# Encoder layer on one core: turned softmax weights kept in the score buffers, value products in fours, and later delayed pieces

## The chip, the cores and the metric

One Trainium2 chip, of which one core is used. The metric is device time in microseconds (us), from the start to the end of one execution; three runs of the kernel before gave 1165.29, 1167.19 and 1170.32 us, median 1167.19.

## What is computed

One layer of a bidirectional encoder on 1024 tokens of width 1024. The combined projection feeds two groups of heads, whose outputs are joined and projected; a gated feed-forward part with a per-layer input follows. The change lies in the two groups of heads alone.

```python
u = einsum('bsd,de->bse', x, w_in)
rq, rk, rv, rg, aq, ak, av = split(u)
y_ret = retention(rq, rk, rv, forward and backward decay) -> group norm * gain * silu(rg)   # 8 heads of 64
y_att = windowed_gqa(aq, ak, av, sink)                                                     # 8 heads, 2 kv heads
mix = concat(y_ret, y_att) @ w_out
h = layer_norm(alpha * x + mix)
out = layer_norm(alpha * h + (silu(h @ w_gate) * (h @ w_up)) @ w_down + sigmoid(h @ w_pg) * (p @ w_pe))

# windowed_gqa, for each block of 128 queries and its up to 3 neighbouring blocks of keys
scores = q k / 8 - slope * distance, masked to |distance| <= 128
m = max(scores, sink);  e = exp(scores - m);  denom = sum(e) + exp(sink - m)
y = (e / denom) @ v
```

## The kernel before, in words

**Products.** Every float32 product is made of three matmuls with operands that are split into an upper and a lower part (`mm3`, lines 82 to 84). One such step of 128x512 is called a projection step below.

**The mixers.** After a first stretch that loads x and makes the first four columns of projection tiles, the kernel works on four pairs of retention heads and four pairs of attention heads (one attention head of each kv group, g = 0 and 1). Round 0 is attention pair 0 beside 80 projection steps, and then retention pair 0 beside 48. Rounds 1, 2 and 3 each hold retention pair i and attention pair i beside 48 projection steps; 16 steps with the last value products end the mixers.

**What sets the order.** TensorE's order is written out by hand: `run` goes through a list in which F stands for a share of the projection steps in `queue` (2 or 3 steps in rounds 1 to 3), and every other entry is a section of mixer work. `take` counts the steps; the count is called ticks. Pieces in `later` and `side` are issued when their tick has come: parts of the group norm (`LAGS`: spread, power, store, fetch, scaled), parts of the softmax sums (`LAGA`), and the pieces that split weights of later stages ahead of time (`presplit_gate`, `presplit_out`, `presplit_small`), each a ScalarE copy, one or two VectorE operations and a store. VectorE, ScalarE and the queue of transfers on SyncE are put in order by the scheduler of the tile framework; `behind` keeps a piece from being scheduled ahead of the matmul after which it was issued.

**Attention, by block n of 128 queries.**
- `scores(n)`: for each g two matmuls into a bank of the kind "s" (lines 579, 580), a VectorE operation that adds bias, takes the row minimum and frees the bank (L581), a ScalarE exponential with its row sum (L584). After blocks 3 and 7, `sums` finishes the denominators of four blocks (L591 to L593).
- `turn(n)`: transposes of the weights into a bank of the kind "t" (L619) and a ScalarE copy (L624) into a buffer `ptr`, of which there are four; the turn of block 2 (or 6), g = 1, also transposes the reciprocals of the sums (L622), from where `spread` sends them through device memory and back into `y` (L604, L608).
- `values(n)`: up to six matmuls (L636) into a bank of the kind "o". After block 3 (or 7) VectorE multiplies the bank by what lies in `y` (L639).

**Retention, by pair i.** `keys` transposes and scales keys (L420, L426), `kv` makes the states' increments in two banks of the kind "t" and then two of the kind "s" (L441), which ScalarE and VectorE free (L450, L448); `scan` adds them up on VectorE (L458) and sends them to the tile `states` (L469); `scores` fills both "s" banks (L480), which VectorE frees by a multiplication into the buffer `pt` (L483), the one from which the backward states are sent; `queries` is L494, `out` lines 506 and 511, `norm` lines 530 to 551.

There are two banks of each kind, used in turn. So a section that fills "s" banks waits until the section before it that did so has been freed.

## Time and profile before

| | |
|---|---|
| three runs, median (lowest to highest) | 1167.19 us (1165.29 to 1170.32) |
| the profiled execution | 1168.1 us |
| its span, first to last instruction | 1166.3 us |
| granted TensorE clock, mean | 0.998 |
| TensorE busy | 1151.7 us, 99% |
| VectorE busy | 896.7 us, 77% |
| ScalarE busy | 565.0 us, 48% |
| mixers (from the first attention scores to the last value products) | about 55 to 344 us |

A row of the timeline has the start in us from the span's start, the length, the engine (PE is TensorE, DVE VectorE, ACT ScalarE, SPq the queue of transfers), the line, the operation, what is written and read, the shape, and the count; in brackets stands the engine's idle time before it and what ended it. Matmuls overlap, so the pitch from one start to the next says what one costs, not its length.

### The profile page before, as it was taken

How to read it: one execution, taken by the hardware profiler on the slowest of the kernel's cores; microseconds unless marked ns; L12 is line 12 of the kernel's file. 1: busy time of each engine (PE TensorE's matmuls, PEld its weight loads, DVE VectorE, ACT ScalarE, POOL GpSimd, SP SyncE). 2: the span in 40 equal slices, each digit the busy share in tenths (PEclk: the TensorE clock that was granted, in tenths of full speed). 3: DMA queues.
4: the chain of work that ended last, by engine and by line, in shares of the span. 5: the costliest groups of instructions: out<-in, count | busy, mean ns of one | idle time of the engine just before them, and what ended most of it. 6: DMA issues, size and time to landing. Idle time of an engine off the chain costs nothing.

```text
span 1166.3 us, 19077 instructions
## 1 busy us (share of the span) xinstructions
PE 1151.7 (99%) x6978; PEld 966.6 (83%) x6978; DVE 896.7 (77%) x1687; ACT 565.0 (48%) x1162; POOL 103.8 (9%) x118
## 2 busy tenths in 40 slices
PE   9999999999999999999999999999999999999997
PEld 7888877878888888888888888888888888888885
DVE  4656678785959898948999988888888976774777
ACT  5655366767646265214445433443344445552462
POOL 2000010101010020000000000000000011133242
PEclk9999999999999999999999999999999999999999
DMA  7345776666467955766232332232223289999978
GB/s 251 89 169 212 255 250 219 232 203 204 144 221 242 360 182 183 267 199 208 108 103 98 107 116 96 96 136 100 100 73 136 87 252 344 335 246 215 258 169 233
DMA packets 88863, 218.64 MB, mean 187 GB/s; under 512 B 12544, under 2 KB 20928, under 8 KB 88768
## 3 DMA queue, kind: packets, MB, share of 16 engines
q1 hardware_dynamic: 79984, 200.11, 49.5%
q0 software_dynamic: 8784, 17.31, 8.4%
q8 instruction: 55, 0.90, 0.3%
q14 instruction: 40, 0.33, 0.1%
HBM read 143.35 MB, written 62.19 MB: 176 GB/s over the span
## 4 chain that ended last, share of the span: by engine, by line
PE 92%; DMA 3%; DVE 2%; issue 1%; SPq 0%; ACT 0%; POOL 0%; DVEq 0%; ACTq 0%; POOLq 0%
PE bmm L876 8%; PE bmm L877 8%; PE bmm L878 8%; PE bt L876 6%; PE bt L877 6%; PE bt L878 6%; PE bmm L82 5%; PE bmm L83 5%; PE bmm L84 5%; PE bs L877 4%; PE bs L878 4%; PE bs L876 4%; PE bo L878 4%; PE bo L877 4%; PE bo L876 4%; PE bo L636 2%
## 5 line engine op out<-in xcount | busy, mean ns | idle before, releaser
L82 PE MATMUL bmm<-H,w 128*128 128x512 f32 x240 | 97.4, 406 | 0.2
L83 PE MATMUL bmm<-H,w 128*128 128x512 f32 x240 | 94.3, 393 | 0.0
L84 PE MATMUL bmm<-H,w 128*128 128x512 f32 x240 | 94.0, 392 | 0.0
L1476 ACT ACTIVATE ev<-ev 128x512 f32<-128x512 f32 x42 | 26.4, 630 | 105.4 <-DVE ev L1505 92.1
L1650 POOL DMA_DIRECT2D h0b<-in_w_dn x24 | 21.6, 900 | 538.5 <-DVE ev L1456 503.6
L82 PEld LDWEIGHTS bmm<-H,w 128*128 128x128 f32 x240 | 45.1, 188 | 11.7 <-issue 1.2
L84 PEld LDWEIGHTS bmm<-H,w 128*128 128x128 f32 x240 | 45.2, 188 | 10.2
L83 PEld LDWEIGHTS bmm<-H,w 128*128 128x128 f32 x240 | 45.3, 189 | 7.7
L584 ACT ACTIVATE sc<-sc,st 128x384 f32<-128x384 f32 (+1 forms) x64 | 37.3, 586 | 18.7 <-DVE st L581 18.5
L624 ACT ACTIVATE ptr<-bt 128x384 f32<-128x384 f32 (+1 forms) x64 | 26.6, 459 | 29.8 <-PE bt L619 29.7
L581 DVE CUSTOM_DVE_ANT_0 sc<-cst,bs,nskb 128x384 f32<-128x384 f32 (+1 forms) x64 | 35.2, 577 | 7.3 <-PE bs L580 7.0
L1505 DVE TENSOR_TENSOR ev<-ev,bt 128x512 f32<-128x512 f32 x44 | 30.1, 683 | 12.5 <-PE bt L878 12.5
L77 DVE TENSOR_TENSOR w<-raw,w 128x512 fp32r<-128x512 f32 x34 | 23.3, 696 | 19.0 <-ACT w L76 18.7
L1456 DVE TENSOR_TENSOR ev<-ev,bs 128x256 f32<-128x256 f32 x63 | 25.6, 418 | 15.5 <-PE bs L878 14.7
L1478 DVE TENSOR_TENSOR ev<-ev 128x512 f32<-128x512 f32 x42 | 29.0, 691 | 10.5 <-ACT ev L1476 9.0
L876 PE MATMUL bmm<-H,u 128*128 128x512 f32 x92 | 36.1, 392 | 0.0
L877 PE MATMUL bmm<-H,u 128*128 128x512 f32 x92 | 36.0, 392 | 0.0
L878 PE MATMUL bmm<-H,u 128*128 128x512 f32 x92 | 35.8, 389 | 0.0
L876 PE MATMUL bmm<-H,w 128*128 128x512 f32 x84 | 32.9, 392 | 0.0
L877 PE MATMUL bmm<-H,w 128*128 128x512 f32 x84 | 32.9, 392 | 0.0
L878 PE MATMUL bmm<-H,w 128*128 128x512 f32 x84 | 32.7, 389 | 0.0
L1456 DVE TENSOR_TENSOR ev<-ev,bo 128x256 f32<-128x256 f32 x70 | 28.4, 417 | 5.1 <-PE bo L878 4.4
(832 smaller groups left out, 3837.1 us busy)
## 6 DMA issues: line engine op xcount, KB each, us to landing
ad<-ev SPq DMA_DIRECT2D x33, 512.0 KB, 2.6
pgd<-pro SPq DMA_DIRECT2D x28, 512.0 KB, 3.5
raw<-in_w_gu SPq DMA_DIRECT2D x22, 512.0 KB, 4.0
ln<-in_w_gu SPq DMA_DIRECT2D x22, 512.0 KB, 4.5
raw<-ad SPq DMA_DIRECT2D x40, 256.0 KB, 6.1
ln<-ad SPq DMA_DIRECT2D x37, 256.0 KB, 6.5
H<-in_w_dn SPq DMA_DIRECT2D x33, 256.0 KB, 9.1
wod<-aq SPq DMA_DIRECT2D x16, 512.0 KB, 3.0
```

Source lines behind the costliest of these rows:

```text
L82: pe.matmul(o, lh, rh, start=start, stop=False)
L83: pe.matmul(o, lh, rl, start=False, stop=False)
L84: recent[0] = pe.matmul(o, ll, rh, start=False, stop=stop).ins.name
L581: dve.tensor_tensor_reduce(sc[g][:, :nk], cst[:, tc0:tc0 + nk], b[:, :nk], slope(i, g), nskb[:, 2 * i + g:2 * i + g + 1], ALU.add, ALU.min ...
L584: act.activation(sc[g][:, :nk], sc[g][:, :nk], AF.Exp, bias=st_[:, 0, j, g:g + 1], scale=-1.0, accum_out=st_[:, 2, j, g:g + 1])
L624: act.activation(p_[:, :hi - lo, :], tb[:, :hi - lo, :], AF.Copy)
L876: pe.matmul(o, lh, rh, start=start, stop=False, skip_group_check=True)
L877: pe.matmul(o, lh, rl, start=False, stop=False, skip_group_check=True)
L878: pe.matmul(o, ll, rh, start=False, stop=stop, skip_group_check=True)
L1456: dve.tensor_tensor(out_, x, b, ALU.add)
L1478: dve.tensor_tensor(c[:, 1, :], c[:, 0, :], c[:, 1, :], ALU.mult)
L1505: dve.tensor_tensor(get(name), ev[left][:, m, :], right, ALU.add)
```

## The change

Five things are done together.

1. `turn` copies the turned weights back into the buffers of the scores (`self.sc`) from which they were transposed; the buffers `ptr` go, and `NSC` doubles from 4 to 8.
2. Value products stand four blocks together, twice for a pair of heads, where they stood two by two four times. Blocks 4 to 7 are multiplied in the next round, ahead of `kv`. The other entries are set out anew: the first scores now come right behind `kv`, without projection steps between, and the scores of block 4 right behind the retention scores. Round 1, which has no value products to take over, has one more share F.
3. The reciprocals are transposed in the turn of block 3 (or 7), g = 0, one block later, and their fetch follows after 4 ticks instead of 5. The multiplication L639 becomes a piece of `later`, 5 ticks behind the value products (`LAGV`).
4. `scaled` (L551) of retention pair 0 comes 4 ticks later (`LAGX`).
5. Seven pieces of `presplit_gate` start at tick 58.5 instead of 57, and the pieces of `presplit_out(2)` move from ticks 7 to 27.4 to ticks 10 to 28.

```diff
-NSC = 4
-LAGA = (2, 1, 5)
+NSC = 8
+LAGA = (2, 1, 4)
 LAGS = (3, 6, 9, 12, 15)
+LAGX = 4
+LAGV = 5
...
-            later.extend((ticks[0] + at, f) for at, f in zip(LAGS, (spread, power, store, fetch, scaled)))
+            late = 0 if self.i else LAGX
+            later.extend((ticks[0] + at, f) for at, f in zip(LAGS, (spread, power, store, fetch)))
+            later.append((ticks[0] + LAGS[4] + late, scaled))
...
-                last = g and n % 4 == 2
+                last = not g and n % 4 == 3
...
-                p_ = bt([P, 3, P], "ptr", 4)
+                p_ = self.sc[n][g].rearrange("p (k q) -> p k q", q=P)
...
             if j == 3:
-                dve.tensor_tensor(self.half(hh), self.o[hh], self.half(hh), ALU.mult)
+
+                def times():
+                    behind(dve.tensor_tensor(self.half(hh), self.o[hh], self.half(hh), ALU.mult))
+
+                later.append((ticks[0] + LAGV, times))
...
-        at = [2 + 2.8 * k for k in range(14)] + [57 + 2.6 * k for k in range(7)] + [75.5] + [79.5 + 2.4 * k for k in range(7)]
+        at = [2 + 2.8 * k for k in range(14)] + [58.5 + 2.5 * k for k in range(7)] + [75.5] + [79.5 + 2.4 * k for k in range(7)]
...
-                side.extend(presplit_out(2, ops, 2, 3.4, late[:1]))
+                side.extend(presplit_out(2, ops, 2, (10, 13, 16, 19, 22, 25, 28), late[:1]))
...
-            run([K(0), F, K(1), *([] if V else [F]), sco(0), F, *V, C(0), C(1), F, sco(1), S_(0, 0), F, trn(0), sco(2), S_(0, 1), F, trn(1),
-                 sco(3), S_(1, 0), F, val(0), val(1), S_(1, 1), F, trn(2), sco(4), F, trn(3), sco(5), Q(0), F, val(2), val(3),
-                 (r.scores,), F, trn(4), sco(6), Q(1), F, trn(5), sco(7), F, (r.out,), E(0), E(1), F, G[0], F, M(0), G[1], F,
-                 val(4), val(5), G[2], F, trn(6), M(1), F, trn(7), F], 48)
-            V = [val(6), val(7)]
+            run([K(0), F, K(1), F, *([] if V else [F]), *V, C(0), C(1), sco(0), F, sco(1), S_(0, 0), F, trn(0), sco(2), S_(0, 1), F,
+                 trn(1), sco(3), S_(1, 0), F, trn(2), S_(1, 1), F, trn(3), Q(0), F, val(0), val(1), val(2), val(3),
+                 (r.scores,), sco(4), Q(1), F, sco(5), F, trn(4), sco(6), F, trn(5), sco(7), F, (r.out,), E(0), E(1), F, G[0], F,
+                 M(0), G[1], F, trn(6), G[2], F, trn(7), M(1), F], 48)
+            V = [val(4), val(5), val(6), val(7)]
```

The list of round 0 is rearranged in the same manner. In the rows of the changed kernel below, lines are up to 8 higher than before (L480 is L482, L483 is L485, L579 is L583, L636 is L640).

**First place: TensorE at the retention scores of round 1.** The retention scores fill the two "s" banks (2063 and 2064 before, 2003 and 2004 after). Before, two projection steps and a turn stand behind them:

```order
L480 MATMUL bs_2063<-rq_1465,rk_1206 64x64
L480 MATMUL bs_2064<-rq_1465,rk_1206 64x64
L82 MATMUL bmm_2039<-H_96,w_1669 128x512
L83 MATMUL bmm_2039<-H_96,w_1669 128x512
L84 MATMUL bmm_2039<-H_96,w_1669 128x512
L82 MATMUL bmm_2039<-H_165,w_1669 128x512
L83 MATMUL bmm_2039<-H_165,w_1669 128x512
L84 MATMUL bmm_2039<-H_165,w_1669 128x512
L619 MATMUL bt_2105<-cst,sc_1978 128x128 x3
L619 MATMUL bt_2111<-cst,sc_1979 128x128 x3
L579 MATMUL bs_2119<-k_411,aq_468 128x384
```

and after the change the scores of block 4 follow at once, in the next use of the same two banks:

```order
L482 MATMUL bs_2003<-rq_1449,rk_1190 64x64
L482 MATMUL bs_2004<-rq_1449,rk_1190 64x64
L583 MATMUL bs_2042<-k_411,aq_468 128x384
L584 MATMUL bs_2042<-kz_413,aq_468 128x384
L583 MATMUL bs_2046<-k_412,aq_1577 128x384
L584 MATMUL bs_2046<-kz_414,aq_1577 128x384
L84 MATMUL bmm_2056<-H_96,w_1653 128x512
```

What moved: all work that lay between filling both banks and needing them again now stands behind the second use. Rounds 2 and 3 have the same order there.

**Second place: VectorE ahead of freeing those banks, round 1.** These are the last rows before the two multiplications that free the banks (`qq`, `rb` and `kv` are scaled queries, `pre` and `pro` pieces of `presplit_gate`). Before:

```order
L656 TENSOR_TENSOR pro_1139<-pre_1134,pro_1139 128x512
L494 TENSOR_TENSOR qq_2025<-rq_1379,qd_1602 128x512 x2
L717 TENSOR_TENSOR pre_1135<-pre_1135,pre_1134 128x512
L494 TENSOR_TENSOR rb_2129<-rq_1465,qd_1602 128x512
L494 TENSOR_TENSOR kv_2130<-rq_1465,qd_1602 128x512
L245 COPY rq_2034<-bmm_1921 64x512
L483 TENSOR_TENSOR pt_2062<-bs_2063,dt_1603 128x512
L656 TENSOR_TENSOR pro_1138<-pre_1135,pro_1138 128x512
L483 TENSOR_TENSOR pt_2062<-bs_2064,dt_1603 128x512
```

and after, where the last wide step of the backward scan (`pt` from `pt`, 128x7x64) stands close ahead too:

```order
L460 SCALAR_TENSOR_TENSOR pt_1769<-pt_1769,cd 128x7x64
L664 TENSOR_TENSOR pro_1122<-pre_1118,pro_1122 128x512
L496 TENSOR_TENSOR qq_1957<-rq_1363,qd_1586 128x512
L725 TENSOR_TENSOR pre_1118<-pre_1119,pre_1118 128x512
L496 TENSOR_TENSOR rb_2052<-rq_1449,qd_1586 128x512
L496 TENSOR_TENSOR kv_2053<-rq_1449,qd_1586 128x512
L664 TENSOR_TENSOR pro_1123<-pre_1118,pro_1123 128x512
L247 COPY rq_1974<-bmm_1900 64x512
L485 TENSOR_TENSOR pt_2002<-bs_2003,dt_1587 128x512
L485 TENSOR_TENSOR pt_2002<-bs_2004,dt_1587 128x512
```

What moved: the four evictions of attention scores that stood between that scan step and the multiplications are gone from there, and seven wide operations lie between.

**Third place: TensorE behind `kv` in round 2.** The last matmuls of `kv` fill the "s" banks (2541 and 2542 before, 2494 and 2493 after). Before, three projection steps follow:

```order
L441 MATMUL bs_2541<-rv_449,pt_2439 64x64 x2
L441 MATMUL bs_2542<-rv_449,pt_2439 64x64 x2
L82 MATMUL bmm_2450<-H_232,w_2269 128x512
L83 MATMUL bmm_2450<-H_232,w_2269 128x512
L84 MATMUL bmm_2450<-H_232,w_2269 128x512
```

and after, the scores of block 0:

```order
L443 MATMUL bs_2493<-rv_449,pt_2390 64x64 x2
L443 MATMUL bs_2494<-rv_449,pt_2390 64x64 x2
L583 MATMUL bs_2531<-k_411,aq_2283 128x256
L584 MATMUL bs_2531<-kz_413,aq_2283 128x256
L583 MATMUL bs_2535<-k_412,aq_2284 128x256
L584 MATMUL bs_2535<-kz_414,aq_2284 128x256
```

What moved: the scores of block 0, which stood ahead of `kv` with a share of projection steps behind them, now take the banks that `kv` has just filled.

More of the change, by code (lines that the diff above doesn't have):

```diff
@@ L803, in layer @@
         run([F, F, sco(0), F, sco(1), F], 16)
-        run([F, (av_turn, 0), (av_turn, 1), F, trn(0), sco(2), F, trn(1), sco(3), F, val(0), val(1), trn(2), sco(4), F,
-             trn(3), sco(5), F, val(2), val(3), trn(4), sco(6), F, trn(5), sco(7), F, val(4), val(5), trn(6), (decay_q, 0),
-             F, trn(7), (decay_k, 0, 0), F, val(6), val(7), (decay_k, 0, 1), F], 64)
-        assert not side and not later
+        run([F, (av_turn, 0), (av_turn, 1), F, trn(0), sco(2), F, trn(1), sco(3), F, trn(2), F,
+             trn(3), F, val(0), val(1), val(2), val(3), sco(4), F, sco(5), F, trn(4), sco(6), F, trn(5), sco(7), F, trn(6), (decay_q, 0),
+             F, trn(7), (decay_k, 0, 0), F, val(4), val(5), val(6), val(7), (decay_k, 0, 1), F], 64)
+        assert not side
         y0 = ytile(0)
```

## The prediction

> **What bounds the kernel now.** I read the page first, then TensorE's waits, then stretches of 10 us over the mixers, then the timeline at each wait.
>
> ```profile
> PE 1151.7 (99%) x6978; PEld 966.6 (83%) x6978; DVE 896.7 (77%) x1687; ACT 565.0 (48%) x1162; POOL 103.8 (9%) x118
> PE bs L579 <- DVE st L581: 3.3, 3, 2.1
> PE bt L622 <- DVE st L593: 1.4, 1, 1.4
> PE bt L441 <- ACT pt L426: 0.7, 1, 0.7
> 180.00:190.00 10.00, 8.04 (x57) 6.26 (x56) 9.24 (x27) 6.83 (x19) 0.00 (x0) 1.00 0.64 221
> 190.00:200.00 10.00, 9.36 (x122) 7.62 (x121) 10.00 (x24) 5.80 (x16) 0.00 (x0) 1.00 0.85 281
> 230.00:240.00 10.00, 7.90 (x158) 6.66 (x155) 6.70 (x14) 5.16 (x14) 0.00 (x0) 1.00 0.58 193
> ```
>
> TensorE is the bound: busy 99% of the span. The change adds no matmul and takes none away. It can win only TensorE's idle time in the mixers, 3.3 + 1.4 + 0.7 = 5.4 us, and the loss where TensorE goes from one kind of section to another. In the stretches (the columns after the length are PE, PEld, DVE, ACT, POOL, clock, DMA share, GB/s) VectorE is full exactly where TensorE waits in round 1: 9.24 and 10.00 of 10 us. Around 235 us it isn't (6.70).
>
> **Joints between sections.** Projection steps run at an even pitch; these rows give what a value section costs beside its matmuls.
>
> ```profile
> 190.28 0.40 PE L82 MATMUL bmm<-H,w 128*128 128x512 f32 x1
> ...
> 191.67 0.82 PE L619 MATMUL bt<-cst,sc 128*128 128x128 f32 x6
> 213.48 0.40 PE L82 MATMUL bmm<-H,w 128*128 128x512 f32 x1
> ...
> 215.64 1.53 PE L636 MATMUL bo<-ptr,av 128*64 128x128 f32 x24
> 217.10 0.50 PE L82 MATMUL bmm<-H,w 128*128 128x512 f32 x1
> ...
> 218.62 0.82 PE L619 MATMUL bt<-cst,sc 128*128 128x128 f32 x6
> 229.31 1.31 PE L636 MATMUL bo<-ptr,av 128*64 128x128 f32 x20
> 230.56 0.64 PE L441 MATMUL bt<-rv,qq 64*64 64x64 f32 x28
> ```
>
> Six matmuls ahead of a turn take 191.67 - 190.28 = 1.39 us, 0.23 each. Nine ahead of values take 215.64 - 213.48 = 2.16, 0.07 over nine such pitches. Twenty-four value matmuls take 1.46 and twenty 1.25, so four cost 0.21, all 24 would cost 1.26, and 0.20 goes at the exit. The six behind them take 1.52, 0.13 too many. A value section thus costs 0.07 + 0.20 + 0.13 = 0.40 us by itself. There are 16 and there will be 8: 3.2 us saved. Against it, 8 turns now end in projection steps and no longer in scores; no row shows this alone, so I bound it by nothing and by the 0.13 above, 1.0 us in all, and take the middle, since the scores then save part of their own entry. Sum: **-2.6 us** (-2.0 to -3.2).
>
> **The waits of before.** There are five.
>
> ```profile
> 170.76 0.45 PE L441 MATMUL bt<-rv,qq 64*64 64x64 f32 x14 [0.67 <-ACT pt L426]
> 179.04 0.75 DVE L551 SCALAR_TENSOR_TENSOR y<-y,gn,rb 128x512 f32<-128x512 f32 x1 [2.26 <-DMA rb<-rnd]
> 181.91 0.44 PE L579 MATMUL bs<-k,aq 128*128 128x384 f32 x1 [0.58 <-DVE st L581]
> 189.47 0.27 PE L622 MATMUL bt<-cst,st 128*8 128x128 f32 x1 [1.38 <-DVE st L593]
> 193.48 0.45 PE L579 MATMUL bs<-k,aq 128*128 128x384 f32 x1 [0.64 <-DVE st L581]
> ```
>
> The 0.67 goes: round 1 gets a share of projection steps ahead of `kv`. The 0.58 came from VectorE, which had stood 2.26 us before L551 for a fetch; 4 ticks of three matmuls at 0.23, 2.8 us, cover that. The 1.38 goes because the reciprocals are transposed a turn later; late next is the same reciprocal, by 0 to 0.5 us. The 0.64 goes because the scores of block 4 no longer come there. Sum: **-3.3 us** (-2.8 to -3.3). The fifth is another matter.
>
> ```profile
> 233.16 0.68 DVE L448 COPY pt<-bs 128x512 f32<-128x512 f32 x1
> ...
> 236.50 0.08 DVE L581 DVE_READ_ACCUMULATOR2_ANT st<- 128x1 f32 x1
> ...
> 237.25 0.45 PE L579 MATMUL bs<-k,aq 128*128 128x384 f32 x1 [2.10 <-DVE st L581]
> q8 instruction: 1, 0.02, 3.8%
> ```
>
> The bank that this matmul takes had been read out by 233.84, and the VectorE operation that the row names ended 0.67 us ahead of the matmul, where the other waits end within 0.1 us of theirs. In the stretch from 234.5 to 236 us a packet of the instruction queue moves (last row; from 230.4 to 234.5 there was none), just behind `kv` with its dense small matmuls. I read it as TensorE short of instructions. The change leaves `kv` where it is but puts the scores, with a wait of their own, into the time in which the instructions come. So it may go or stay: 0 to -2.1, and I take half, **-1.0 us**. The Trainium skill (Runtime: NRT & Kernel Launch, section Instruction fetch mechanics) says that instructions come in blocks of 256 and that crossing a block is "mostly hidden". By that the wait would be VectorE's after all and would go whole, and the sum would be 1.1 us lower; the trace speaks against it with the bank free since 233.84.
>
> **New wait 1: scores right behind `kv`.** In the three rounds block 0 now needs banks that `kv` has just filled.
>
> ```profile
> 172.66 0.50 PE L82 MATMUL bmm<-H,w 128*128 128x512 f32 x1
> ...
> 172.84 0.55 ACT L450 ACTIVATE pt<-bs 128x448 f32<-128x448 f32 x1 [0.30 <-PE bs L441]
> 172.85 0.69 DVE L448 COPY pt<-bs 128x512 f32<-128x512 f32 x1 [0.28 <-PE bs L441]
> ```
>
> `kv` was over at 172.66, and the banks were free at 173.39 and 173.54. The wait is 0.73 with both engines idle; it was hidden by projection steps and now stands open. With 0.05 for the signal: 3 x 0.8 = **+2.4 us** (2.2 to 3.6, the upper end being 0.4 more each, from the copy that came late at 233.16).
>
> **New wait 2: scores right behind the retention scores.** Block 4 needs the two banks that L483 has to free.
>
> ```profile
> 316.03 0.50 PE L82 MATMUL bmm<-H,w 128*128 128x512 f32 x1
> ...
> 316.15 1.29 DVE L483 TENSOR_TENSOR pt<-bs,dt 128x512 f32<-128x512 f32 x2 [0.51 <-PE bs L480]
> 191.61 0.68 DVE L458 SCALAR_TENSOR_TENSOR pt<-pt,cd 128x448 f32<-128x448 f32 x1
> 192.31 1.11 SPq L469 DMA_DIRECT2D states<-pt  x2
> DMA to landing us min/median/max: 3.1/3.3/6.2
> 195.62 1.29 DVE L494 TENSOR_TENSOR qq<-rq,qd 128x512 f32<-128x512 f32 x2
> 196.82 0.69 DVE L717 TENSOR_TENSOR pre<-pre,pre 128x512 f32<-128x512 f32 x1
> ```
>
> With VectorE idle, the second bank is free at 317.44, 1.41 us after the retention scores; the first half of the attention scores fills 0.35 of this (two matmuls of 384 columns, against 0.23 for 512). The floor is 1.1 us a round. But L483 writes the buffer `pt` out of which the backward states are sent, and that is now late. From the end of that scan step (192.29) the two issues take until 193.42, and 3.3 us (median) later the second has landed: 4.5 us. Before, L483 came 7 to 9 us behind the scan step. Now four blocks of values (2.5 us) and the retention scores (1.1) follow a last share of steps, and by the order on VectorE (pitch 0.60 for a wide operation, 196.82 - 195.62 halved) I count the scan's end at about 3.3 us before the retention scores' end in rounds 2 and 3, with two to four wide operations behind it. So L483 starts 1.2 us late: 1.1 + 1.0 = 2.1 each. In round 1 seven wide operations stand between scan and L483: 4.2 us. VectorE has 15 wide and 9 narrow operations, 10.6 us, between the eviction of block 3 and L483, and TensorE's sections take 10.5, with VectorE some 1.6 us behind at their start: L483 starts 1.6 to 1.9 us late, a wait of 2.8. Sum 2.8 + 2.1 + 2.1 = **+7.0 us** (3.3 at the floor; about 12 if transfers take 5 us to land, between median and maximum).
>
> **Costed at nothing.** Copying turned weights in place is the same ScalarE work, and the buffers are as many, 8; block 4's scores need block 0's values, which stand ahead on TensorE itself. The later multiplication L639 covers its fetch in rounds 1 to 3; uncovered, it would hold VectorE some 1 us (included in the range). The 16 last steps still cover the pieces behind the mixers.
>
> **Sum.** -2.6 - 3.3 - 1.0 + 2.4 + 7.0 = +2.5 us. Against the profiled execution (span 1166.3, and 1.8 around it: 1168.1) that is 1170.6; the median of the runs is 0.9 lower, so I say **1169.7 us**: no difference that can be measured, since a measurement of this kernel can tell about 0.5%, 5.8 us, from no change.
>
> **The rivals.**
> - *Floors.* If the states land in time, both new waits stay at their floors, 2.2 + 3.3, and the fifth wait goes: -2.6 - 3.3 - 2.1 + 5.5 = -2.5, 1164.7 us. For it speaks that VectorE has slack over a round; against it the 4.5 us from scan to landing.
> - *Late states, slower than before.* If the transfer of the backward states binds in all three rounds at 5 us rather than 3.3, by stores of pieces ahead of it on the queue (round 1 has 0.85 DMA share at 190 to 200), wait 2 is 12 us and the sum +7.5: 1174.7. It decides from a wait of 3.4 us a round on.
> - *The clock.* TensorE starts slow:
>
> ```profile
> 6.02 0.63 PE L82 MATMUL bt<-H,w 128*128 128x512 f32 x1
> 6.45 0.63 PE L82 MATMUL bo<-H,w 128*128 128x512 f32 x1
> ...
> 7.52 0.39 PE L83 MATMUL bs<-H,w 128*128 128x512 f32 x1
> 7.75 0.40 PE L84 MATMUL bs<-H,w 128*128 128x512 f32 x1
> ```
>
> Its pitch is 0.43 until about 6.9 us and 0.23 after, some 5.6 us of slow work from 1.3 us on. If the wait in round 1 sent it back to that state, 5.6 x (1 - 0.23/0.43) = 2.6 us would come on top: 1172.3. A wait of 2.10 us left the clock at 1.00. The Trainium skill (TensorE: Matmul & The Clock Gate, section Why this matters for your kernels) warns of gaps over about 3 us; no wait here was that long.
> - *It doesn't do what it says.* The three waits for VectorE (2.6) only move: 1172.3.
>
> **Chances.** Forecast 0.55, floors 0.20, late states 0.18, clock 0.04, moved waits 0.03. Faster by over 0.5% 0.03 (the lower edge of the floors), slower 0.20 (late states, and half of the last two rounded), the same 0.77. The range goes from 1163.5 (floors, with joints at -3.2 and half a us of spread) to 1177 (late states with the fifth wait kept).
>
> **What would show it.** In the changed profile: L441 and L622 gone from TensorE's waits (terms of -3.3); 16 value sections become 8; a wait of 0.8 before the first L583 behind L443 in each round; a wait of about 2 to 3 before L583 behind L482, with L485 started late by a transfer of `states`. A floor wait of 1.1 there, or waits over 4, would prove the main term wrong.

## The result, and the profile after

| | before | after |
|---|---|---|
| median of the runs (lowest to highest) | 1165.13 us (1164.79 to 1170.32), 6 runs | 1182.76 us (1181.18 to 1186.25), 6 runs |
| the profiled execution | 1168.1 us | 1181.43 us |
| its span | 1166.3 us | 1179.7 us |
| granted clock, mean | 0.998 | 0.993 |

The ratio is 1.0147, with a 95% interval of 1.0134 to 1.016: the change makes the kernel slower by about 17 us, where 1169.7 us and no measurable difference had been forecast, and the time lies above the range. The profiled executions differ by 13.3 us, since that of before is 3.0 us above its median and that of after 1.3 us below; this account is made with these two.

First the busy line of the page of after:

```profile
PE 1155.0 (98%) x6978; PEld 970.6 (82%) x6978; DVE 896.1 (76%) x1687; ACT 563.7 (48%) x1162; POOL 103.5 (9%) x118
```

and TensorE's largest waits in the mixers of after (engine, what is written, line, the releaser; us in total, times, longest):

```profile
PE bs L583 <- DVE pt L485: 9.2, 3, 3.4
PE bt L626 <- DVE st L597: 2.4, 2, 1.4
PE bs L583 <- ACT pt L452: 2.2, 3, 0.7
PE bt L443 <- ACT pt L428: 0.5, 1, 0.5
PE bt L623 <- ACT sc L628: 0.4, 1, 0.4
```

TensorE has as many matmuls as before, yet is busy 3.3 us longer: some of them ran more slowly. The forecast's two new waits are there, in three rounds each. The first (L452, the copies behind `kv`) was forecast at 2.4 us in all and has 2.2; the second (L485) at 7.0 and has 9.2. The wait for the reciprocals (L626), which was to go, is longer than before: 2.4 us in all, where it was 1.4.

The timeline of after at the three long waits, with what VectorE did: the last row of the backward scan (in round 1 also the transfer's issue, SPq, and VectorE's last operation ahead of the multiplications), the two multiplications that free the banks, the scores of block 4. Rows between are left out.

```profile
191.28 0.67 DVE L460 SCALAR_TENSOR_TENSOR pt<-pt,cd 128x448 f32<-128x448 f32 x1
192.09 1.21 SPq L471 DMA_DIRECT2D states<-pt  x2
195.49 0.68 DVE L247 COPY rq<-bmm 64x512 f32<-64x512 f32 x1
197.43 1.29 DVE L485 TENSOR_TENSOR pt<-bs,dt 128x512 f32<-128x512 f32 x2 [1.27 <-DMA states<-pt]
198.17 0.58 PE L583 MATMUL bs<-k,aq 128*128 128x384 f32 x1 [3.44 <-DVE pt L485]
...
253.00 0.68 DVE L460 SCALAR_TENSOR_TENSOR pt<-pt,cd 128x448 f32<-128x448 f32 x1
258.76 1.29 DVE L485 TENSOR_TENSOR pt<-bs,dt 128x512 f32<-128x512 f32 x2 [1.89 <-DMA states<-pt]
259.50 0.49 PE L583 MATMUL bs<-k,aq 128*128 128x384 f32 x1 [2.42 <-DVE pt L485]
...
316.21 0.68 DVE L460 SCALAR_TENSOR_TENSOR pt<-pt,cd 128x448 f32<-128x448 f32 x1
322.90 1.29 DVE L485 TENSOR_TENSOR pt<-bs,dt 128x512 f32<-128x512 f32 x2 [4.80 <-DMA states<-pt]
323.64 0.44 PE L583 MATMUL bs<-k,aq 128*128 128x384 f32 x1 [3.34 <-DVE pt L485]
```

and the transfers of the tile `states`, from issue to landing:

```profile
DMA to landing us min/median/max: 3.9/4.5/5.2
```

In all three rounds VectorE stood idle ahead of L485, for 1.27, 1.89 and 4.80 us, and the transfer of the backward states out of `pt` ended it: the mechanism of the forecast. In rounds 2 and 3 VectorE was free before the retention scores were done. In round 1 it was late too: it came free at 196.17 us (195.49 + 0.68), 1.4 us behind TensorE's last retention score (198.17 - 3.44 = 194.73), and stood 1.27 us more for the transfer. But the states took longer. From the end of the scan (the start of its row and its length) to the start of L485 it is 5.5, 5.1 and 6.0 us; 4.5 had been counted, with 3.3 us for a transfer. That was the median of before, where the trace has the landing of six of the 16 transfers. In after it has four, and their median is 4.5.

What the forecast's sum lacks shows when the span is cut into stretches of 3.41 us. The columns are the stretch, its length, TensorE's busy time and instructions, the granted clock, DMA share and GB/s. First after, at the three waits, then before, around its wait of 2.10 us:

```profile
194.91:198.32 3.41, 0.15 (x1) 1.00 1.01 351
198.32:201.73 3.41, 3.41 (x10) 0.50 0.40 117
201.73:205.14 3.41, 3.41 (x19) 1.00 0.47 160
...
256.35:259.76 3.41, 0.99 (x53) 1.00 0.86 272
259.76:263.17 3.41, 3.41 (x10) 0.50 0.70 189
...
321.20:324.61 3.41, 0.97 (x4) 1.00 0.06 12
324.61:328.02 3.41, 3.41 (x10) 0.50 0.26 78
```

```profile
232.53:235.94 3.41, 2.61 (x12) 1.00 0.46 178
235.94:239.35 3.41, 2.10 (x11) 1.00 0.62 229
```

Behind each of the three waits TensorE had half its clock for one stretch of 3.41 us: ten matmuls, against 19 in the full stretch that follows the first one. From the start of the first matmul behind the wait to the start of the 31st it is 7.40, 7.77 and 7.91 us, against 6.08, 6.36 and 6.36 in the run with the scans swapped below, which has the same order of matmuls and no such stretch: 4.3 us in all.

So the 13.3 us of the profiled executions are: waits of TensorE before the output projection 14.7 us instead of 5.4, +9.3; half clock +4.3; joints -1.7 (not measured one by one: it is what is left of the 11.87 us by which the output projection starts later, next rows); and 1.5 us behind the mixers.

```profile
354.68 0.39 PE L876 MATMUL bt<-w,H 128*128 128x512 f32 x1
366.55 0.39 PE L884 MATMUL bt<-w,H 128*128 128x512 f32 x1
```

### The profile page after: what moved, and what is told of

Its sections match the earlier page's. It is cut to its first block, busy times and chain, and to the rows that moved or that the text cites. A ratio compares the mean times of both kernels' runs of the same rounds, so it can differ in the third digit from the quotient of the medians.

```text
span 1179.7 us, 19068 instructions
## 1 busy us (share of the span) xinstructions
PE 1155.0 (98%) x6978; PEld 970.6 (82%) x6978; DVE 896.1 (76%) x1687; ACT 563.7 (48%) x1162; POOL 103.5 (9%) x118
## 4 chain that ended last, share of the span: by engine, by line
PE 67%; DMA 2%; DVE 1%; SPq 0%; issue 0%; ACT 0%; POOL 0%; DVEq 0%; POOLq 0%
PE bmm L884 8%; PE bmm L885 8%; PE bmm L886 8%; PE bt L884 6%; PE bt L885 6%; PE bt L886 6%; PE bs L886 4%; PE bs L885 4%; PE bs L884 4%; PE bo L886 4%; PE bo L885 4%; PE bo L884 4%; DMA rnd<-sn 1%; DMA sn<-rb 0%; DVE acc L1759 0%
## 5 line engine op out<-in xcount | busy, mean ns | idle before, releaser
L86 PEld LDWEIGHTS bmm<-H,w 128*128 128x128 f32 x240 | 46.2, 192 | 10.6
L84 PEld LDWEIGHTS bmm<-H,w 128*128 128x128 f32 x240 | 46.1, 192 | 10.6 <-ACT H L78 0.9
L85 PEld LDWEIGHTS bmm<-H,w 128*128 128x128 f32 x240 | 46.3, 193 | 8.1
L585 DVE CUSTOM_DVE_ANT_0 sc<-cst,bs,nskb 128x384 f32<-128x384 f32 (+1 forms) x64 | 35.0, 576 | 13.5 <-PE bs L584 13.1
L1464 DVE TENSOR_TENSOR ev<-ev,bs 128x256 f32<-128x256 f32 x63 | 25.5, 417 | 15.6 <-PE bs L886 14.7
L1486 DVE TENSOR_TENSOR ev<-ev 128x512 f32<-128x512 f32 x42 | 29.0, 691 | 10.5 <-ACT ev L1484 9.0
L628 ACT ACTIVATE sc<-bt 128x384 f32<-128x384 f32 (+1 forms) x64 | 27.2, 455 | 15.7 <-PE bt L623 10.5
L583 PE MATMUL bs<-k,aq 128*128 128x384 f32 (+1 forms) x64 | 23.3, 369 | 11.3 <-DVE pt L485 9.2
```

The source lines that it names most:

```text
L84: pe.matmul(o, lh, rh, start=start, stop=False)
L85: pe.matmul(o, lh, rl, start=False, stop=False)
L86: recent[0] = pe.matmul(o, ll, rh, start=False, stop=stop).ins.name
L585: dve.tensor_tensor_reduce(sc[g][:, :nk], cst[:, tc0:tc0 + nk], b[:, :nk], slope(i, g), nskb[:, 2 * i + g:2 * i + g + 1], ALU.add, ALU.min ...
L628: act.activation(p_[:, :hi - lo, :], tb[:, :hi - lo, :], AF.Copy)
L1486: dve.tensor_tensor(c[:, 1, :], c[:, 0, :], c[:, 1, :], ALU.mult)
```

## The experiments

Each was timed against the kernel before on the same chip; ratios are to before, with 95% intervals. For after itself the ratio is 1.0147. Where single waits are named, they are of the one profiled execution.

### Work in the place of the long waits

```diff
+            def filler():
+                b = bank("o")
+                for _ in range(10):
+                    pe.matmul(b, xs[0][:, 0, 0:P], xs[0][:, 0, 0:HF], start=True, stop=True)
...
-                 (r.scores,), sco(4), Q(1), F, sco(5), ...
+                 (r.scores,), (filler,), sco(4), Q(1), F, sco(5), ...
```

> After, with ten matmuls of 128x512 (their product is used by nothing) put between the retention scores and the scores of block 4 in rounds 1 to 3: about 2.2 us of TensorE work in the place of each of the three waits on L485. Nothing that the waits wait for is changed. Theory of the clock (each of these waits sends TensorE to half its granted clock for one stretch of 3.4 us, about 1.7 us lost each): the waits fall from 3.44, 2.42 and 3.34 us to about 1.2, 0.2 and 1.1, no slice of the trace shows a granted clock under 0.9 there, and the time falls by about 5 us against after (span about 1174.6 us). Rival 1 (the drops come from somewhere else, or cost nothing): the work stands where the wait stood, and the time is that of after within 1 us. Rival 2 (the waited-for chain itself hangs on TensorE): the waits stay as long and the time grows by about 6 us.

Measured: 1177.94 us, 1.0106 (1.0091 to 1.0121), 4.8 us below after, with 30 matmuls more. The waits are 1.35, 0.63 and 0.84 us, and the clock stays up. In round 1, where after has half clock from 198.32 us, two stretches of 4 us:

```profile
194.00:198.00 4.00, 3.22 (x62) 1.00 1.00 317
198.00:202.00 4.00, 3.43 (x16) 1.00 0.42 137
```

TensorE does useless work instead of standing still, the states leave as before (in round 1 their issue starts at 192.01 us, in after at 192.09), and the kernel is faster. Both rivals fall, and of what the traces show only the clock accounts for the gain. So these drops cost about 5 us of the 17.6, by the medians. The two profiled executions lie only 1.9 us apart: that of this run is its slowest of four, with 0.77 us of standing at 237.00 us that nothing in the profile explains.

### One projection step between

```diff
-                 (r.scores,), sco(4), Q(1), F, sco(5), ...
+                 (r.scores,), F, sco(4), Q(1), F, sco(5), ...
```

> After, with one projection step (as before the change) between the retention scores and the scores of block 4 in rounds 1 to 3, and so one step less at each round's end. Theory (the waits on L485 and the drops of the clock behind them are 14.3 us of the 17.6 that the change costs by the medians; in before the step covers 2.0 us or so of each): the waits fall to about 1.8, 0.8 and 1.7 us, no drop of the clock, time about 9 to 10 us below after, near 1172. Rival (states arrive as much later as the step takes, since the order on VectorE hangs on TensorE): waits of 2.4 us or more stay, the clock drops stay, and less than 3 us is gained.

Measured: 1172.26 us, 1.0048 (1.003 to 1.0067), 10.5 us below after. The waits are 0.78, 1.01 and 2.10 us, and the rival falls. One expectation missed: the 2.10 us of round 3 did bring a half-clock stretch, though the 2.10 us of before had not.

```profile
316.99:320.40 3.41, 1.69 (x7) 1.00 0.41 130
320.40:323.81 3.41, 3.41 (x10) 0.50 0.01 2
```

Here 1.72 us of the wait fell into one stretch; in before the border at 235.94 cut the wait into 0.80 and 1.30 (its rows above). More on this at the end.

### The scans in the other order

```diff
-... sco(1), S_(0, 0), F, trn(0), sco(2), S_(0, 1), F, trn(1), sco(3), S_(1, 0), F, trn(2), S_(1, 1), F, trn(3), Q(0), F, val(0), ...
-                 (r.scores,), sco(4), Q(1), F, ...
+... sco(1), S_(1, 0), F, trn(0), sco(2), S_(1, 1), F, trn(1), sco(3), S_(0, 0), F, trn(2), S_(0, 1), F, trn(3), F, val(0), ...
+                 (r.scores,), sco(4), Q(0), Q(1), F, ...
```

> After, with the two scans in the other order in rounds 1 to 3: the backward scan first, the forward one in its place, and the first query-decay product (which reads the forward scan's states) behind the scores of block 4. The sections of TensorE keep their order; only what VectorE has to do ahead of the instruction of L485 is changed: the states of the scan that block 4's buffer waits for leave some 6 us earlier. Theory of the late transfer (L485's first write waits until the states have left the buffer that it overwrites): the waits on L485 fall from 3.44, 2.42 and 3.34 us to under 1.5 each, with none or one drop of the clock, and the time falls by 6 to 10 us against after. Rival (VectorE is late in itself, since its queue is full at that place): the waits stay at 2.4 us or more each, the time within 2 us of after.

Measured: 1170.41 us, 1.0041 (1.0026 to 1.0056), 12.4 us below after, more than expected. VectorE and TensorE at the same place in rounds 1 and 3:

```profile
195.28 1.29 DVE L485 TENSOR_TENSOR pt<-bs,dt 128x512 f32<-128x512 f32 x2 [0.42 <-PE bs L482]
196.03 0.45 PE L583 MATMUL bs<-k,aq 128*128 128x384 f32 x1 [0.85 <-DVE pt L485]
...
314.25 1.29 DVE L485 TENSOR_TENSOR pt<-bs,dt 128x512 f32<-128x512 f32 x2 [3.45 <-PE bs L482]
315.00 0.44 PE L583 MATMUL bs<-k,aq 128*128 128x384 f32 x1 [0.80 <-DVE pt L485]
```

TensorE's order is that of after, instruction for instruction. The backward states leave earlier, and VectorE has the first query product (two wide operations) behind L485 and no longer ahead of it. L485 now begins as soon as the retention scores are there: its releaser is L482, no longer the transfer. The waits are down to the time of one multiplication, 0.85, 0.85 and 0.80 us. So the late transfer made the waits of rounds 2 and 3 long, and a full VectorE did not: there it stood idle in after before the retention scores were done. Round 1 is mixed: of its 3.44 us VectorE's own work took 1.4 and the transfer 1.27, and this run, which takes load off VectorE too, doesn't part them. There is no half clock in this trace. Against before it has on top the three waits for L452, 0.8 us a round, and 2.5 us behind the mixers; the old waits have stayed, but for the one of 2.10 us.

### One projection step between `kv` and the scores

```diff
-            run([K(0), F, ..., *V, C(0), C(1), sco(0), F, ...
+            run([K(0), F, ..., *V, C(0), C(1), F, sco(0), F, ...
```

> After, with one projection step between the retention's second kv part and the scores of block 0 in rounds 1 to 3 (one step less at each round's end). Theory of the prediction (new wait 1: the scores' banks are not free yet, 0.70, 0.72 and 0.72 us): these three waits go, one joint more in each round costs some 0.06 us each, and the time falls by about 2 us against after. Rival (the wait goes to the next place that needs ScalarE's exponentials): the wait on L452 or L443 comes back behind it, and the time stays within 0.7 us.

Measured: 1177.2 us, 1.0098 (1.0083 to 1.0113), 5.6 us below after: more than either theory gave. The waits for L452 are gone, but the next rows show what rose for them:

```profile
PE bs L583 <- DVE pt L485: 6.3, 3, 3.2
PE bt L626 <- DVE st L597: 3.4, 3, 1.7
PE bt L623 <- ACT sc L628: 1.6, 1, 1.6
PE bt L443 <- ACT pt L428: 1.2, 1, 1.2
PE bs L583 <- DVE st L585: 0.8, 1, 0.8
```

L626, L623, L443 and L585 together went up from 3.3 to 7.1 us and took back more than the 2.2 that L452 gave. The gain is elsewhere: round 3's long wait fell from 3.34 to 1.35, one of the half-clock stretches went (two are left), and 1.3 us of it lie behind the mixers. So the rival was right on these waits, and neither was right on the time: the theory's 2 us fell short, and the gain came from places that neither had named.

### Both places mended, and what is then late

With this, both new waits should go while the value sections stay together:

```diff
-            run([K(0), F, K(1), F, *([] if V else [F]), *V, C(0), C(1), sco(0), F, sco(1), S_(0, 0), ...
+            run([K(0), F, K(1), F, *V, sco(0), F, C(0), C(1), F, sco(1), S_(0, 0), ...
-                 (r.scores,), sco(4), Q(1), F, sco(5), F, trn(4), sco(6), ...
+                 sco(4), F, sco(5), F, trn(4), (r.scores,), Q(1), F, sco(6), ...
```

> After, with the order of rounds 1 to 3 mended at the two places where waits arose: the value section goes ahead of block 0's scores and a projection step stands between kv and block 1's scores; the scores of blocks 4 and 5 and block 4's turn stand ahead of the retention scores, so that no attention scores follow these directly. Theory (the change costs what these two places cost; its fewer joints are worth 2 to 2.6 us): the waits on L452 and on L485 are gone or under 0.5 us each, no drop of the clock, the waits on L626 (some 2.4 us in all) stay, and the time is 1 to 3 us below the kernel before (ratio 0.9975 to 0.999). Rival (VectorE and ScalarE are full in these stretches, so a wait taken away at one place comes back at the next): waits of 5 us or more in all stay in rounds 1 to 3 at other lines, and the time is that of before or up to 5 us more.

Measured: 1167.76 us, 1.0013 (1.0005 to 1.0022). 15 of the 17.6 us are gone, by order alone: most of the change's cost sat at these two places and in the clock behind them. The rest of the theory missed, and the rival has it: 5.6 us of waits are left before the output projection, at other lines (next rows: a ScalarE wait and what TensorE lost by it; a VectorE wait and what TensorE lost by that).

```profile
183.15 0.63 ACT L663 ACTIVATE pro<-pre 128x512 fp32r<-128x512 f32 x1 [2.68 <-DMA pgd<-pro]
186.78 0.44 PE L623 MATMUL bt<-cst,sc 128*128 128x128 f32 x2 [2.14 <-ACT sc L628]
...
234.08 0.75 DVE L553 SCALAR_TENSOR_TENSOR y<-y,gn,rb 128x512 f32<-128x512 f32 x1 [1.37 <-DMA rb<-rnd]
236.22 0.44 PE L583 MATMUL bs<-k,aq 128*128 128x384 f32 x1 [0.79 <-DVE pt L450]
```

In round 1 a piece of the gate's split stood at the head of ScalarE's queue until its buffer had been written out, with block 3's exponentials behind it. In round 2 the scaling L553 stood at the head of VectorE's queue until its factors had come, with the copy L450 behind it. (It is the scaling of retention pair 1; the change delays pair 0's alone.) After has the first of these as well, 1.26 us on ScalarE, 1.46 on VectorE behind it, and then the late reciprocal:

```profile
183.87 0.63 ACT L663 ACTIVATE pro<-pre 128x512 fp32r<-128x512 f32 x1 [1.26 <-DMA pgd<-pro]
184.54 0.69 DVE L664 TENSOR_TENSOR pro<-pre,pro 128x512 fp32r<-128x512 f32 x1 [1.46 <-ACT pro L663]
188.15 0.19 DVE L597 RECIPROCAL st<-st 128x8 f32<-128x8 f32 x1
```

The next run puts the reciprocals' transposition one head later in that order:

```diff
-                last = not g and n % 4 == 3
+                last = g and n % 4 == 3
```

> The run before this one (waits covered), with the reciprocals' transposition behind the second head's transposes of blocks 3 and 7 instead of the first head's, some 0.8 us later on TensorE. Theory (L626 waits only because the reciprocal on VectorE, L597, comes late by up to 1.4 us): the waits on L626 fall by 0.7 to 0.8 us each, 1.2 to 1.5 us in all, and the time by as much. Rival (the first head's transposes wait for ScalarE's exponential anyway, L623 on L628): a wait as long appears there and the time stays within 0.5 us.

Measured: 1169.7 us, 1.0031 (1.0019 to 1.0043), slower by 2 us. The waits for L626 fell from 1.4 to 0.3 us, but those on L623 rose from 2.1 to 3.0, and the 2.05 us of round 1 brought a half-clock stretch. Neither expectation held as to the time. The rows above put the cause of the wait on L623 further back, with ScalarE; the runs with other times for the split, below, test that.

The same with the delayed pieces taken back:

```diff
-LAGA = (2, 1, 4)
-LAGX = 4
+LAGA = (2, 1, 5)
+LAGX = 0
...
-... + [58.5 + 2.5 * k for k in range(7)] + ...
+... + [57 + 2.6 * k for k in range(7)] + ...
...
-                side.extend(presplit_out(2, ops, 2, (10, 13, 16, 19, 22, 25, 28), late[:1]))
+                side.extend(presplit_out(2, ops, 2, 3.4, late[:1]))
```

> The run with the later reciprocals, with the delayed pieces taken back (the retention's scaling 4 steps later, the broadcast a step earlier, the split's starts in rounds 0 and 2): the order of TensorE is the same. Theory of the prediction (the delayed pieces cost nothing and gain only what lies beside the 2.10 us wait at 237 us of before, about 1 us): 0 to 2 us slower than with them. Rival (the delays put work behind the mixers, 1.5 us of the 13.3 of the profiled difference): 1 to 2 us faster than with them.

Measured: 1168.09 us, 1.0014 (1.0004 to 1.0023), 1.6 us faster than with them. L623 in round 1 falls from 2.05 to 0.27 + 0.80 us, and the wait for L450 rises from 0.68 to 1.71. The rival's number came, but not for its reason alone: of the 1.4 us between the two traces up to the last matmul, 0.6 lie before the output projection and 0.8 behind it.

And the delayed pieces without the rest of the change (a diff to before), TensorE's order that of before:

```diff
+LAGX = 4
...
-            later.extend((ticks[0] + at, f) for at, f in zip(LAGS, (spread, power, store, fetch, scaled)))
+            late = 0 if self.i else LAGX
+            later.extend((ticks[0] + at, f) for at, f in zip(LAGS, (spread, power, store, fetch)))
+            later.append((ticks[0] + LAGS[4] + late, scaled))
...
-... + [57 + 2.6 * k for k in range(7)] + ...
+... + [58.5 + 2.5 * k for k in range(7)] + ...
...
-                side.extend(presplit_out(2, ops, 2, 3.4, late[:1]))
+                side.extend(presplit_out(2, ops, 2, (10, 13, 16, 19, 22, 25, 28), late[:1]))
```

> The kernel before, with only the delayed pieces that work there (the retention's scaling 4 steps later in rounds 1 to 3, the split of the gate and of the output weights at the later times): TensorE's order is that of before. Theory of the prediction (at most the 2.10 us wait at 237 us moves): 0 to 1 us below before (ratio 0.999 to 1.000). Rival (these pieces cost what appears behind the mixers): 1 to 2 us above before (ratio 1.001 to 1.002).

Measured: 1167.74 us, 1.0016 (1.0003 to 1.0029), the rival's number again. (The expectation says that the scaling is later in rounds 1 to 3; it is so for pair 0 alone, in round 1.) Its runs go from 1165.43 to 1172.79, and the profiled one is the fastest of them: it has no wait at 237 us and none of the rival's loss behind the mixers. What makes the others slow isn't shown.

### Curing what is late next

Three runs with the order that has both waits covered: the seven pieces of the split in round 1 back at the times of before; spread wider; and, with the times of before, the scaling 7 steps later.

```diff
-... + [58.5 + 2.5 * k for k in range(7)] + ...
+... + [57 + 2.6 * k for k in range(7)] + ...
```

> The order with both waits covered, with the split of the gate's weights in round 1 back at the times of before (57 + 2.6k in place of 58.5 + 2.5k). In that order's trace ScalarE stood 2.68 us at 183 us in a piece of this split, whose buffer was still being written out, with block 3's exponentials queued behind it; TensorE then waited 2.14 us (L623). Theory (the old waits stayed in the change because its delayed pieces of the split hold up ScalarE in round 1): that wait falls to 0.5 us or less, the time by 1.5 to 2.5 us, to the time of before or up to 1 us below it (ratio 0.999 to 1.000). Rival (another piece stands at that place then): the wait moves, and the time stays within 0.7 us.

Measured: 1166.63 us, 1.0007 (0.9997 to 1.0016). The 2.14 us wait is gone, as the theory has it; the time fell by 1.1 us rather than 1.5 or more, since the wait for L450 grew to 1.40.

```diff
-... + [58.5 + 2.5 * k for k in range(7)] + ...
+... + [57 + 3.0 * k for k in range(7)] + ...
```

> The same with the round's seven pieces of the split spread wider (57 + 3.0k), so that each finds its buffer written out. Theory: as in the run with before's times, or up to 0.5 us better, with ScalarE's idle time ahead of these pieces under 1 us each. Rival (the round's later pieces then meet the retention scores' scaling instead): L485 waits of 1 us or more in round 1, and the time 1 us above that run.

Measured: 1165.51 us, 1.0 (0.9991 to 1.0009). ScalarE's waits ahead of these pieces are 0.55 us or less but for one of 0.99, and L485 costs 0.24 in round 1. The theory's sign, with 1.1 us where 0.5 was expected; the two intervals overlap.

```diff
-LAGX = 4
+LAGX = 7
```

> The run with the split's times of before, with the retention's scaling 3 steps later still (7 in place of 4). In the covered order's trace VectorE stood 1.37 us at 233 us in this scaling (L553, its factors still on the way), with the kv product's copy behind it, and TensorE waited 0.79 us (L583 on L450). Theory (the scaling is still too early for its transfer): that wait goes, 0.5 to 1 us in all, and the ratio to before falls under 1.000. Rival (VectorE is full there without it): the wait stays within 0.3 us and so does the time.

Measured: 1164.07 us, 0.9989 (0.9979 to 0.9998). The time falls as the theory has it, the wait doesn't go, and the edit shows why: `late = 0 if self.i else LAGX` moves the scaling of pair 0, and the one at the start of round 2 is pair 1's. It still stands there:

```profile
229.88 0.75 DVE L553 SCALAR_TENSOR_TENSOR y<-y,gn,rb 128x512 f32<-128x512 f32 x1 [1.28 <-DMA rb<-rnd]
232.02 0.44 PE L583 MATMUL bs<-k,aq 128*128 128x384 f32 x1 [0.69 <-DVE pt L450]
```

What moved lies in round 1. There the first scaling went from 178.90 to 184.55 us, and the reciprocal (L597) now stands ahead of it, at 184.23 instead of 185.53; the wait of 0.53 for it is gone. The place named in the expectation was wrong. (Not all of the 2.6 us is explained: the wait for L450 is also shorter, 0.69 us against 1.40, though its scaling was not moved.)

Both cures at once:

```diff
-LAGX = 4
+LAGX = 7
...
-... + [58.5 + 2.5 * k for k in range(7)] + ...
+... + [57 + 3.0 * k for k in range(7)] + ...
```

> Both at once: the order with the waits covered, the split's pieces spread wider (57 + 3.0k), and the retention's scaling 7 steps later. Theory (the two cures are of different waits: the split's of ScalarE in round 1, the scaling's of VectorE at the start of round 2): the waits of rounds 1 to 3 together are 2.0 to 2.5 us, and the time is 0 to 0.6 us below that of the run with the scaling later, ratio to before 0.998 to 0.999. Rival (these two hold the same place up): the time of the run with the scaling later, or up to 1 us above it.

Measured: 1164.93 us, 0.9984 (0.9975 to 0.9993). By the ratio this is the fastest of all, better than before by 0.16% and than after by 1.6%; the intervals don't tell it apart from the run with the scaling later. Its profiled execution was the slowest of its 11, with a wait for L450 of 1.39 us, so its 3.8 us of waits before the output projection, against 2.0 to 2.5 expected, say little of the median.

The same with the scalings of pairs 1 and 2 later too:

```diff
-            late = 0 if self.i else LAGX
+            late = (LAGX, 4, 4, 0)[self.i]
```

> The run with both cures, with the scaling of retention pairs 1 and 2 also later, by 4 steps: the change delays pair 0's alone, and the scaling in which VectorE stood 1.28 to 1.99 us at 229 to 233 us, in front of the kv copy, is pair 1's. Theory (that standing makes the wait for L450): VectorE's idle time ahead of that scaling falls to under 0.5 us, the wait of TensorE on L450 goes, and the time falls by 0.5 to 1 us, ratio to before 0.9975 to 0.998. Rival (the later scaling then meets the scores of round 2, as in round 1): a wait as long appears on another line before 260 us, and the time stays within 0.4 us.

Measured: 1164.4 us, 0.9991 (0.9982 to 1.0). VectorE no longer stands ahead of this scaling, the copy L450 goes ahead of it, and no wait for L450 is left:

```profile
229.67 0.69 DVE L450 COPY pt<-bs 128x512 f32<-128x512 f32 x1 [0.23 <-PE bs L443]
233.89 0.75 DVE L553 SCALAR_TENSOR_TENSOR y<-y,gn,rb 128x512 f32<-128x512 f32 x1
```

The theory of that wait is right. But the reciprocals' waits of rounds 2 and 3 went from 0.33 and 0.64 us to 0.69 and 1.32, and by the intervals the time isn't another: the rival holds as to the time. The last three runs lie 0.1 to 0.2% below before, this one with an interval that reaches 1.0; which of them is best isn't settled.

### The split's old times in after itself

```diff
-... + [58.5 + 2.5 * k for k in range(7)] + ...
+... + [57 + 2.6 * k for k in range(7)] + ...
```

> After, with nothing changed but the times of the split's seven pieces in round 1, back at those of before (57 + 2.6k). Theory (in after, too, the old wait for the reciprocals in round 1 stays since the delayed pieces hold up ScalarE and with it VectorE): the wait on L626 in round 1 falls from 1.38 to under 0.6 us, and the time falls by about 1 us against after (ratio near 1.0138). Rival (the reciprocals are late in the new order by themselves): L626 in round 1 stays at 1 us or more, and the time within 0.4 us of after.

Measured: 1181.4 us, 1.0143 (1.0127 to 1.0159), by the ratios 0.5 us below after, which the intervals don't tell from nothing. ScalarE stands longer, not shorter, ahead of such a piece, and TensorE loses 2.8 us in round 1 in place of 1.4:

```profile
183.06 0.63 ACT L663 ACTIVATE pro<-pre 128x512 fp32r<-128x512 f32 x1 [2.79 <-DMA pgd<-pro]
184.61 0.93 PE L623 MATMUL bt<-cst,sc 128*128 128x128 f32 x6 [1.60 <-ACT sc L628]
189.42 0.27 PE L626 MATMUL bt<-cst,st 128*8 128x128 f32 x1 [1.18 <-DVE st L597]
```

So the theory falls for after: its new times are not what keeps the old waits. In after's order such a piece meets block 3's exponentials at either set of times.

## Why the prediction was wrong

| step of the sum | forecast, us | profile of after, us |
|---|---|---|
| joints | -2.6 | -1.7 |
| four waits of before | -3.3 | +0.1 |
| fifth wait | -1.0 | -2.1 |
| new wait 1 (kv to scores) | +2.4 | +2.2 |
| new wait 2 (retention scores to scores) | +7.0 | +9.2 |
| half clock | not in the sum | +4.3 |
| behind the mixers | 0 | +1.5 |
| sum | +2.5 | +13.5 (rounded terms; measured 13.3) |

The two sums are 11.0 us apart: 4.3 by the clock, 3.4 by the old waits, 2.2 by new wait 2, 1.5 behind the mixers and 0.9 by the joints, less 1.1 for the fifth wait and 0.2 for new wait 1.

**The clock: a rival with a chance of 0.04 came true in all three rounds.** The step that failed is the sentence "A wait of 2.10 us left the clock at 1.00 ... no wait here was that long". One wait without a drop was taken for a safe length. What counts here is how much of the wait falls into one stretch of the clock's grid (last section): of those 2.10 us no more than 1.30 did. The three stretches cost 4.3 us by the pitches of the matmuls and 4.8 by the run with work in the waits, and the forecast's price for one, 2.6 us, was too high (1.3 to 1.6 measured). The mechanism was there, with a wrong condition.

**New wait 2: right in kind, short by 2.2 us.** The order on VectorE was read rightly: in rounds 2 and 3 the scan ended 3.4 us before the retention scores, 3.3 forecast. The transfer was mis-sized: 5.1 to 6.0 us from the scan's end to L485 in after, 4.5 counted. The 3.3 us in that count was the median of six landings, and the 6.2 beside it in the forecast's own row is the second transfer of round 3's backward states, the place where VectorE stood longest ahead of L485 in after. In round 1 the forecast counted VectorE's own work as the limit, 1.6 to 1.9 us late; it was 1.4 us late, and the transfer added 1.27 on top. This is the mechanism of the rival of the late states, without its size (9.2 of its 12 us). Swapping the scans shows for rounds 2 and 3 that the transfer is the cause; why it took longer than 3.3 us wasn't tested.

**The old waits: the rival that they only move, given 0.03, holds.** They were 3.27 us in before and are 0.50 + 1.38 + 0.43 + 1.02 = 3.33 in after. The reciprocals' wait was to go "because the reciprocals are transposed a turn later", with half a us left at most. By the trace the reciprocal of round 1 waited behind VectorE's part of a split piece, that for ScalarE, and ScalarE for the piece's own transfer. I had costed these pieces without looking at what is queued behind each. With the waits covered, the split's old times took away the wait on ScalarE (2.14 us) and left 0.53 us of the reciprocals'; in after's own order they made both together longer (2.8 us for 1.4). So the order and the times decide it together; why the waits of rounds 2 and 3 stay wasn't tested.

**Joints: the mechanism held, the size not.** -1.7 us, and -1.3 in the trace with the scans swapped, below the smallest forecast of -2.0. Which joint costs more than counted wasn't tested.

**Fifth wait and the end.** The 2.10 us at 237 us are gone from after, and also from the trace with the delayed pieces alone, where TensorE's order is that of before. That speaks against a shortage of instructions that the order fixes; but one execution of each can't settle it, and in the run with work in the waits 0.77 us stand at 237.00 that nothing in the profile explains. What made up the 1.5 us behind the mixers is open too: traces with the same delayed pieces have between 0.1 and 2.5 there (the step between `kv` and the scores, and the swapped scans).

**The 4.3 us between the profiles (13.3) and the medians (17.6).** 3.0 of them are that the profiled execution of before lies above its median; whether the faster ones have its 2.10 us wait too isn't known. The other 1.3 are after's. Its executions have mean clocks of 0.989 (the slowest, 1186.25 us) to 0.994 (the fastest, 1181.18), which fits with more or fewer half-clock stretches; but one of 1184.93 us has 0.993, so that isn't all. Only one trace of each kernel is on record.

## What to carry to other kernels

Before a second use of a bank is moved up to the first, follow the engine that frees it back to every transfer that it must wait for, and price that transfer at its slow end at that moment, since it now stands open. A wait of some 2 us on TensorE has a second price, the clock behind it, and even useless matmuls in its place were cheaper here; better is an order in which the two uses lie apart, or in which the transfer leaves earlier. And look at what is queued behind every piece that waits for a transfer of its own: at the head of its engine's queue it holds up all of it.

## What the hardware showed

The half-clock stretches lie on a fixed grid. In after they begin at 198.32, 259.76 and 324.61 us, 18 and 19 times 3.413 us apart, and each is 3.413 us long. The clock's first rise in that trace, at 7.17 us, lies 56 such lengths ahead of the first of them; in traces without a drop the grid is counted from that rise. In every trace a drop in the mixers follows directly on a stretch of the grid in which TensorE stood idle for about half of it or more (1.56 to 3.27 us). In all 16 traces there were nine grid stretches in the mixers with 1.72 us idle or more, and all nine were followed by half clock. Of the six with 1.44 to 1.71 us one was, and of those below none. That one is in the run with the delays undone: 1.56 us, in three waits of 0.27, 0.80 and 0.49, while a single wait of 1.71 us in the same trace cost nothing. So the length of a wait alone does not decide. In after with the split's old times a wait of 2.84 us was cut by the border into 1.32 and 1.53 and cost no stretch (first two rows: the clock is still 1.00 in the second, and it is so in the next; the 30 matmuls behind it took 6.06 us, against 7.40 in after); a wait of 1.76 that lay in one piece did, in the run with a step between `kv` and the scores (last two).

```profile
193.65:197.07 3.42, 2.10 (x84) 1.00 0.97 266
197.07:200.48 3.41, 1.88 (x8) 1.00 0.77 271
```

```profile
258.16:261.57 3.41, 1.65 (x70) 1.00 0.87 272
261.57:264.98 3.41, 3.41 (x10) 0.50 0.70 196
```

Where the grid lies differs from one execution to the next (the first rise is at 4.16 to 7.29 us in these traces), so the same wait may cost a stretch in one and not in another. The Trainium skill (TensorE: Matmul & The Clock Gate, section What's actually happening) has the window as free-running and 3413 ns long, and these traces agree. The same page of the Trainium skill advises to avoid gaps over about 3 us (section Why this matters for your kernels); these traces don't bear that limit out, since the shortest single wait that cost a stretch was 1.76 us.
